# Fewer, longer runs of plain f32 instructions on TensorE in the token mixers of a two-layer streaming encoder

## The chip, the cores and the metric

The kernel runs on one core of a Trainium2 chip. The metric is the device time of one execution in microseconds (us). The five engines are called by the letters of the profile: PE (TensorE, with PEld for its weight loads), DVE (VectorE), ACT (ScalarE), POOL (GpSimd) and SP (SyncE, which issues most loads here).

## What is computed

The input `x` has 512 rows of 1024 values. There are two layers, each a token mixer and then a channel mixer (a gated MLP with a causal convolution of width 3), each with its residual, and a last norm. Layer A's mixer is an mLSTM of 4 heads (192 wide) beside memory attention; layer B's is band attention of 12 heads (64 wide) over keys and values that both come from layer A's output, beside memory attention. The three parts that the change touches, cut from the reference:

```python
# layer A: mLSTM output hm of each head, normalised over the head's 192 values
hm = hm * lax.rsqrt(jnp.mean(hm * hm, axis=-1, keepdims=True) + EPS)
...
# layer B: band attention of one chunk of 64 queries over 9 chunks of keys
s = jnp.einsum('bqhd,bkhd->bhqk', qc, kc) * scale + bias
p = jax.nn.softmax(jnp.where(valid, s, -jnp.inf), axis=-1)
return jnp.einsum('bhqk,bkhd->bqhd', p, vc)
...
# both layers: memory attention, 4 heads of 64 over 256 memory tokens
s = jnp.einsum('bshd,bmhd->bhsm', q, mk) * (MEM_HEAD_DIM ** -0.5)
return jnp.einsum('bhsm,bmhd->bshd', jax.nn.softmax(s, axis=-1), mv)
...
x = x + jnp.concatenate([mix_out, mem_out], axis=-1) @ w_out
```

## The kernel before, in words

Activations are held transposed: features on the 128 partitions, the 512 tokens along the free axis. A product in f32 is made of three products in the type fp32r: each operand is divided by `split` (L130) into a high part, a cast on ACT, and a low part, a subtraction on DVE, and `mm3` (L164) sums hi·hi, hi·lo and lo·hi, on lines L166, L167 and L168. So each tile of weights or activations that PE is to use passes through ACT and then DVE first. Tiles named `wr`, `wh`, `wl` are a load of weights and its two parts, `u` mostly activations and their parts, `pt` softmax weights in two parts, `t` work tiles, `s` small ones, `pmm`, `psc`, `ptr` the tiles of PSUM (3, 3 and 2 of them).

Some work on PE stays in plain f32: a transpose (L573, L1317) has the identity as one operand, and each mLSTM head has sums of squares against a matrix `mcf` of two columns (L1166, L1167).

The order of work in a mixer is written as generators. `weave(job, filler, each, lead)` takes a step of the job (a head, a pair of heads) and then as many steps of filler (projections, one `mm3` a step) as the job's `yield` has earned: `each` for a bare `yield`, `each` times the number for a numbered one. A scheduler then sets the order on each engine, with program order as priority and its own costs; each engine works in that order and waits where an operand isn't there.

- Memory attention (`memory_attention`, two heads at a time): scores on L504, softmax on L558 to L564 (maximum, exponential, reciprocal, and two normalising multiplies a head), for the first half of the queries and then for the second; `transposed(T2)` makes four transposes and a split for one head, yields, and does the same for the other; then the products with the values (L587, "PV" below) and `values`, L523 and L524, which adds the halves into a tile `t` that a split turns into the `u` pair that the output projection reads.
- Band attention (`band_attention`, six jobs of two heads): softmax of the query block T over T + 1 key blocks on L1302 to L1308, both heads, and `transposed(T)` with T + 1 transposes and a split for one head, then for the other. The steps stand in the order softmax 0, softmax 1, transposed 0, softmax 2, transposed 1, softmax 3, transposed 2, transposed 3, PV on L1338 and L1339.
- mLSTM heads (`mlstm_head`): the squares of both parts of the head go through ACT, four pairs of sums follow with a `yield 0.581` behind each, then a chain of small DVE instructions (L1171 to L1173, `rsqrt` L210, `diagonal` L221), a `yield 2.673`, and `spread` (L241), which PE needs the chain for.

Layer A weaves its four heads and the two pairs of memory attention one after another. Layer B weaves band jobs 0 to 3, memory pair 0, band job 4, and then, with the output projection `outp.part(...)` as filler, memory pair 1 and band job 5.

Of the kernel before, what the change touches and what calls it, by code (L numbers as in the profile page):

```python
# [12 lines left out]
AF = mybir.ActivationFunctionType  # L13
ALU = mybir.AluOpType
AX = mybir.AxisListType

P = 128
# [36 lines left out]
def trunk(  # L54
# [76 lines left out]
    def split(hi, lo, src, on_act=True, pinned=False):  # L131
        high = A.copy(hi, src) if on_act else V.tensor_copy(hi, src)  # L132
        low = V.tensor_tensor(out=lo, in0=src, in1=f(hi), op=ALU.subtract)  # L133
        if pinned:
            pin(high)
            pin(low)

    def load(src, a, b, extra=None):
# [67 lines left out]
    def until(there, filler):  # L206
        while not there():
            next(filler)

    def rsqrt(y, v):  # L210
# [331 lines left out]
    def memory_attention(q, kv, hp, mixes):  # L542
# [4 lines left out]
        ptl = [p[:, 2 * S : 4 * S].rearrange("p (a t) -> p a t", a=2) for p in pts]  # L547
        es = {}

        def softmax(T2):  # L550
# [5 lines left out]
            for h in range(2):  # L556
# [6 lines left out]
                for i in range(2):  # L563
                    V.tensor_scalar(e[:, i, :], e[:, i, :], sm[:, i : i + 1], None, op0=ALU.mult)  # L564
                es[T2, h] = e
                yield

        def transposed(T2):
            for h in range(2):
                tp = ps("tr").rearrange("p (a t c) -> p a t c", a=2, t=2)  # L570
                for i in range(2):
                    for a in range(2):
                        nc.tensor.transpose(tp[:, a, i, :], es[T2, h][:, i, a * P : (a + 1) * P], ident)  # L573
# [534 lines left out]
    def mlstm_head(h):  # L1108
# [48 lines left out]
        for o, j, r in ((nums[0], full, slice(0, P)), (nums[1], sh, rs)):  # L1157
            sq = sb("t", [P, S])
            A.activation(sq, o, AF.Square)
            sqs.append(sq)  # L1160
            V.tensor_tensor(out=og[j][r, :], in0=o[r, :], in1=og[j][r, :], op=ALU.mult)
        yield
        st = ps("sc")
        for T in range(TT):
            sl = slice(T * P, (T + 1) * P)
            nc.tensor.matmul(st[:, 2 * T : 2 * T + 2], sqs[0][:, sl], mcf[:, 0, :], start=True, stop=False)  # L1166
            nc.tensor.matmul(st[:, 2 * T : 2 * T + 2], sqs[1][:, sl], mcf[:, 1 + odd, :], start=False, stop=True)  # L1167
            yield 0.581
        st = st[:, : 2 * TT].rearrange("p (t c) -> p t c", c=2)
# [5 lines left out]
        dg = diagonal(fc)  # L1175
        yield 2.673
        fb = spread(dg, "sc")
# [107 lines left out]
    def band_attention(j, q, k, v):  # L1285
# [9 lines left out]
        def softmax(T):  # L1295
# [3 lines left out]
            for h in range(2):  # L1299
# [7 lines left out]
                V.reciprocal(sm, sm)  # L1307
                V.tensor_scalar(e, e, sm, None, op0=ALU.mult)  # L1308
                es[T, h] = e
            yield  # L1310

        def transposed(T):
            n = (T + 1) * P
            for h in range(2):
                tp = ps("tr")
                for b in range(T + 1):
                    nc.tensor.transpose(tp[:, b * P : (b + 1) * P], es[T, h][:, b * P : (b + 1) * P], ident)  # L1317
# [172 lines left out]
```

## Time and profile before

| | |
|---|---|
| runs, us | 1205.53, 1205.76 (median), 1206.40 |
| profiled execution, us | 1205.96 |
| its span, us | 1204.2 |
| PE, PEld, DVE, ACT, POOL busy share of the span | 99%, 88%, 79%, 58%, 10% |
| plain f32 matmuls of the kinds that the change touches | 360 |
| ACT table loads | 18 |

The span is from the first to the last instruction of the profiled execution; 1.8 us lie outside it. A time in the profile is counted from the start of the span. In a row of the timeline the first number is the start, the second the duration, the sign `x4` says that four like instructions were put together, and brackets give what the engine waited for just before. On PE the duration of a matmul is longer than the distance to the next one, because they overlap; the cost of one is therefore read from the distance of starts.

### The profile page before, as it was taken

The numbers are of one execution on the slowest core, as the hardware profiler recorded it, in microseconds if no ns is written. First come the engines' busy times: TensorE is split into PE (matmuls) and PEld (weight loads), VectorE is DVE, ScalarE is ACT, GpSimd is POOL, SyncE is SP. The second block draws the span as 40 slices with busy tenths as digits, with TensorE's granted clock in tenths as the row PEclk, the third lists the DMA queues.
The fourth block names the chain that finished last, engine by engine and source line by source line (L and its number), as shares of the span: only waits on it lengthen the run. The fifth ranks groups of instructions, "written<-read, shape, count | busy, mean of one in ns | idle before, by whom it ended". The sixth has DMA issues, their size and how long they took to land.

```text
span 1204.2 us, 18753 instructions
## 1 busy us (share of the span) xinstructions
PE 1192.6 (99%) x7047; PEld 1057.7 (88%) x7047; DVE 950.4 (79%) x1737; ACT 704.4 (58%) x1245; POOL 123.4 (10%) x207
## 2 busy tenths in 40 slices
PE   9999999999999999999999999999999999999997
PEld 9988888888889999999988888888889999999986
DVE  7878688778978877777698888997897877777755
ACT  4536577644555555555565667775455555555545
POOL 1300101000021111111020000001001010111100
PEclk9999999999999999999999999999999999999999
DMA  8634211454276666665563323246336466666551
GB/s 277 202 104 119 58 53 57 130 154 132 70 173 161 156 157 156 147 141 131 136 202 114 95 72 93 59 128 202 115 91 145 109 141 137 141 140 137 119 156 70
DMA packets 199020, 156.00 MB, mean 130 GB/s; under 512 B 7864, under 2 KB 179346, under 8 KB 198930
## 3 DMA queue, kind: packets, MB, share of 16 engines
q1 hardware_dynamic: 184338, 120.78, 34.3%
q0 software_dynamic: 14592, 34.03, 14.3%
q8 instruction: 55, 0.90, 0.3%
q14 instruction: 35, 0.29, 0.1%
HBM read 126.27 MB, written 32.44 MB: 132 GB/s over the span
## 4 chain that ended last, share of the span: by engine, by line
PE 93%; ACT 3%; DVE 3%; issue 1%; ACTq 0%; DVEq 0%
PE pmm L166 18%; PE pmm L167 17%; PE pmm L168 17%; PE ptr L166 6%; PE ptr L167 6%; PE ptr L168 6%; PE psc L166 5%; PE psc L167 5%; PE psc L168 5%; PE psc L504 2%; PE ptr L1317 1%; ACT wh L132 1%; PE ptr L1338 1%; PE ptr L1339 1%; ACT t L561 0%
## 5 line engine op out<-in xcount | busy, mean ns | idle before, releaser
L166 PE MATMUL pmm<-u,wh 128*128 128x512 f32 (+1 forms) x968 | 336.6, 348 | 0.1
L168 PE MATMUL pmm<-u,wl 128*128 128x512 f32 (+1 forms) x968 | 333.7, 345 | 0.0
L167 PE MATMUL pmm<-u,wh 128*128 128x512 f32 (+1 forms) x968 | 333.3, 344 | 0.1
L133 DVE TENSOR_TENSOR wl<-wr,wh 128x1024 fp32r<-128x1024 f32 (+4 forms) x174 | 201.9, 1161 | 103.0 <-ACT wh L132 102.4
L132 ACT CAST wh<-wr 128x1024 fp32r<-128x1024 f32 (+4 forms) x174 | 174.0, 1002 | 107.5 <-PE pmm L167 46.9
L168 PEld LDWEIGHTS pmm<-u,wl 128*128 128x128 f32 x968 | 183.6, 190 | 21.1
L167 PEld LDWEIGHTS pmm<-u,wh 128*128 128x128 f32 x968 | 183.9, 190 | 18.3 <-DVE u L133 0.8
L166 PEld LDWEIGHTS pmm<-u,wh 128*128 128x128 f32 x968 | 183.7, 190 | 18.1 <-ACT u L132 0.5
L166 PE MATMUL ptr<-u,wh 128*128 128x512 f32 x272 | 106.7, 392 | 0.0
L167 PE MATMUL ptr<-u,wh 128*128 128x512 f32 x272 | 106.5, 392 | 0.0
L168 PE MATMUL ptr<-u,wl 128*128 128x512 f32 x272 | 105.8, 389 | 0.0
L736 POOL DMA_DIRECT2D xspill<-t x64 | 55.5, 867 | 465.8 <-ACT t L735 455.4
L168 PE MATMUL pmm<-u,u 128*128 128x256 f32 x296 | 84.0, 284 | 0.2 <-DVE u L133 0.2
L166 PE MATMUL pmm<-u,u 128*128 128x256 f32 x296 | 84.2, 285 | 0.0
L167 PE MATMUL pmm<-u,u 128*128 128x256 f32 x296 | 83.8, 283 | 0.0
L133 DVE TENSOR_TENSOR u<-pt,u 128x512 fp32r<-128x512 f32 x102 | 70.2, 688 | 11.8 <-ACT u L132 9.2
L166 PE MATMUL psc<-u,wh 128*128 128x256 f32 (+1 forms) x232 | 76.1, 328 | 0.0
L168 PE MATMUL psc<-u,wl 128*128 128x256 f32 (+1 forms) x232 | 75.9, 327 | 0.0
L167 PE MATMUL psc<-u,wh 128*128 128x256 f32 (+1 forms) x232 | 75.9, 327 | 0.0
L735 ACT COPY t<-ptr 128x512 f32<-128x512 f32 x64 | 37.5, 586 | 60.4 <-PE ptr L168 60.4
L132 ACT CAST u<-pt 128x512 fp32r<-128x512 f32 x102 | 63.1, 619 | 11.4 <-DVE pt L845 11.3
L907 ACT ACTIVATE t<-t 128x512 f32<-128x512 f32 x34 | 21.6, 634 | 79.5 <-DVE t L644 79.5
(282 smaller groups left out, 2524.4 us busy)
## 6 DMA issues: line engine op xcount, KB each, us to landing
wr<-in_ffn_w_up_dram SPq DMA_DIRECT2D x54, 512.0 KB, 5.1
wr<-in_ffn_w_down_dram SPq DMA_DIRECT2D x38, 512.0 KB, 4.0
pt<-in_ffn_w_up_dram SPq DMA_DIRECT2D x34, 512.0 KB, 6.5
xspill<-t POOLq DMA_DIRECT2D x64, 256.0 KB, 4.9
wr<-in_a_w_in_dram SPq DMA_DIRECT2D x20, 512.0 KB, 3.7
xspill<-u POOLq DMA_DIRECT2D x32, 256.0 KB, 3.0
u<-xspill SPq DMA_DIRECT2D x32, 256.0 KB, 5.0
wr<-in_w_kv_dram SPq DMA_DIRECT2D x12, 512.0 KB, 4.0
```

What stands on the lines that cost most here:

```text
L132: high = A.copy(hi, src) if on_act else V.tensor_copy(hi, src)
L133: low = V.tensor_tensor(out=lo, in0=src, in1=f(hi), op=ALU.subtract)
L166: nc.tensor.matmul(o, lh, rh, start=first, stop=False, skip_group_check=more)
L167: nc.tensor.matmul(o, lh, rl, start=False, stop=False, skip_group_check=more)
L168: nc.tensor.matmul(o, ll, rh, start=False, stop=last, skip_group_check=more)
L504: nc.tensor.matmul(o, a, b, start=first and i == 0, stop=i == 1)
L735: A.copy(t, o)
L736: G.dma_start(xspill[j], t, accum_op=ALU.add)
L907: A.activation(self.acc, self.acc, AF.Silu)
L1317: nc.tensor.transpose(tp[:, b * P : (b + 1) * P], es[T, h][:, b * P : (b + 1) * P], ident)
L1338: nc.tensor.matmul(o2[:, s * P :], w, hi_at(pts[h], s, s, TT - s), start=s == 0, stop=False)
L1339: nc.tensor.matmul(o2[:, s * P :], w, lo_at(pts[h], s, s, TT - s), start=False, stop=s == TT - 1)
```

## The change

The instructions are the same, but for two more ACT table loads; their order is not. 84 stretches of plain f32 instructions on PE between fp32r ones become 51.

- `split` gives back its last instruction, and a helper `behind(i, *others)` makes instruction `i` wait for others.
- Memory attention: `transposed(T2)` takes both `ptr` tiles first and makes the eight transposes of both heads in succession; the first waits for the second head's last normalising multiply, and for the last split of the run before.
- Band attention: `transposed` takes several T. T = 0 and T = 1 become one run of both heads (2 · (1 + 2) transposes) behind softmax 2, with a bare `yield` more behind it; T = 2 and T = 3 are a run of both heads each. The first transpose waits for the second head's normalise.
- mLSTM: the eight sums stand in succession and the first waits for the last square; the `yield` behind the chain is 4.997, which is 2.673 + 4 · 0.581.

```diff
         def transposed(T2):
+            tps = [ps("tr").rearrange("p (a t c) -> p a t c", a=2, t=2) for _ in range(2)]
+            run_ = []
             for h in range(2):
-                tp = ps("tr").rearrange("p (a t c) -> p a t c", a=2, t=2)
+                e = es[T2, h][0]
                 for i in range(2):
                     for a in range(2):
-                        nc.tensor.transpose(tp[:, a, i, :], es[T2, h][:, i, a * P : (a + 1) * P], ident)
-                tsl = slice(2 * T2 * P, 2 * (T2 + 1) * P)
-                split(pth[h][:, :, tsl], ptl[h][:, :, tsl], tp.rearrange("p a t c -> p a (t c)"))
+                        run_.append(nc.tensor.transpose(tps[h][:, a, i, :], e[:, i, a * P : (a + 1) * P], ident))
+            behind(run_[0], es[T2, 1][1], *freed)
+            tsl = slice(2 * T2 * P, 2 * (T2 + 1) * P)
+            for h in range(2):
+                last = split(pth[h][:, :, tsl], ptl[h][:, :, tsl], tps[h].rearrange("p a t c -> p a (t c)"))
                 yield
+            freed.append(last)
...
-            nc.tensor.matmul(st[:, 2 * T : 2 * T + 2], sqs[0][:, sl], mcf[:, 0, :], start=True, stop=False)
+            i = nc.tensor.matmul(st[:, 2 * T : 2 * T + 2], sqs[0][:, sl], mcf[:, 0, :], start=True, stop=False)
+            if T == 0:
+                behind(i, last)
             nc.tensor.matmul(st[:, 2 * T : 2 * T + 2], sqs[1][:, sl], mcf[:, 1 + odd, :], start=False, stop=True)
-            yield 0.581
...
-        yield 2.673
+        yield 4.997
...
-        def transposed(T):
-            n = (T + 1) * P
-            for h in range(2):
-                tp = ps("tr")
-                for b in range(T + 1):
-                    nc.tensor.transpose(tp[:, b * P : (b + 1) * P], es[T, h][:, b * P : (b + 1) * P], ident)
-                split(
-                    blocks(pts[h], (T + 1) * P, 640, T + 1), blocks(pts[h], 3 * 640 + T * P, -768, T + 1),
-                    tp[:, :n].rearrange("p (b t) -> p b t", t=P),
-                )
+        def transposed(*Ts):
+            tps = [ps("tr") for _ in range(2)]
+            run_ = []
+            for T in Ts:
+                c = T * P if len(Ts) > 1 else 0
+                for h in range(2):
+                    e = es[T, h][0]
+                    for b in range(T + 1):
+                        run_.append(
+                            nc.tensor.transpose(tps[h][:, c + b * P : c + (b + 1) * P], e[:, b * P : (b + 1) * P], ident)
+                        )
+            behind(run_[0], es[Ts[-1], 1][1])
+            for T in Ts:
+                c = T * P if len(Ts) > 1 else 0
+                for h in range(2):
+                    split(
+                        blocks(pts[h], (T + 1) * P, 640, T + 1), blocks(pts[h], 3 * 640 + T * P, -768, T + 1),
+                        tps[h][:, c : c + (T + 1) * P].rearrange("p (b t) -> p b t", t=P),
+                    )
             yield
...
         yield from softmax(1)
-        yield from transposed(0)
         yield from softmax(2)
-        yield from transposed(1)
+        yield from transposed(0, 1)
+        yield
         yield from softmax(3)
```

Lines move with it: the helper's L166 to L168 become L167 to L169, memory transposes L573 become L583, memory PV L587 becomes L600, `values` L523 and L524 become L531 and L532, band softmax L1302 to L1308 become L1316 to L1322, band transposes L1317 become L1336, the sums L1166 and L1167 become L1179 and L1182, their chain L1171 to L1173 and L213 to L228 becomes L1185 to L1187 and L221 to L236, `spread`'s product L241 becomes L249.

The order changes in three places that are of interest. First, DVE behind the sums of the second mLSTM head: before, the chain's first instructions (on tiles `s`) alternate with taps of the convolution (L1075), and a split of weights stands ahead of them.

```order
L133 TENSOR_TENSOR wl_1875<-wr_1872,wh_1874 128x1024
L1075 SCALAR_TENSOR_TENSOR t_1694<-pmm_1628,cols_535,t_1694 128x511
L1171 TENSOR_TENSOR s_1726<-psc_1691,floor_592 128x4
L1075 SCALAR_TENSOR_TENSOR t_1694<-pmm_1628,cols_535,t_1694 128x510
L1172 TENSOR_SCALAR s_1726<-s_1726 128x4
```

After, in the same place:

```order
L1185 TENSOR_TENSOR s_1700<-psc_1691,floor_592 128x4
L1186 TENSOR_SCALAR s_1700<-s_1700 128x4
L1187 SCALAR_TENSOR_TENSOR s_1700<-psc_1691,s_1700 128x4
L221 TENSOR_SCALAR s_1701<-s_1700 128x4
L133 TENSOR_TENSOR wl_1875<-wr_1872,wh_1874 128x1024
L222 TENSOR_SCALAR s_1701<-s_1701 128x4
```

The taps have left the chain and the split of weights has come into it. On PE, 20 fp32r matmuls stand between the last sum and `spread` of this head after the change.

Second, PE at the end of layer A's memory pair 0, after the change (before, 15 matmuls stood between the last transposes and the first PV product):

```order
L583 MATMUL ptr_1961<-ident,t_1895 128x128 x4
L583 MATMUL ptr_1962<-ident,t_1910 128x128 x4
L167 MATMUL psc_2072<-u_1731,u_1783 128x512
L168 MATMUL psc_2072<-u_1732,u_1783 128x512
L169 MATMUL psc_2072<-u_1731,u_1784 128x512
L1132 MATMUL psc_2084<-u_894,sel_81 128x384
L600 MATMUL ptr_1984<-pt_1803,u_1270 128x512 x2
```

Four matmuls are left there. ACT, ahead of the same place, after the change (before, the two exponentials of L561 stand next to each other, with one table load behind them):

```order
L569 ACTIVATE t_1910,s_1908<-psc_1849,s_1907 128x256
L1089 ACT_TABLE_LOAD
L1089 ACTIVATE t_1854<-t_1854 128x512
L569 ACT_TABLE_LOAD
L569 ACTIVATE t_1910,s_1908<-psc_1849,s_1907 128x256
L493 ACTIVATE u_1860<-t_1854 64x512
L493 ACTIVATE u_1861<-t_1854 64x512
L496 CAST u_1860<-u_1860 64x512
L496 CAST u_1861<-u_1861 64x512
L132 CAST pt_1804<-ptr_1920 128x2x256
```

A silu of the convolution (L1089, on `t_1854`) with its table load, and another load back, have come between the two exponentials of a head; the first run's cast into `pt_1804`, whose split the second run of transposes waits for, stands behind.

Third, memory pair 1 of layer B with band job 5. PE, from the pair's PV to the first use of its result; before, 18 fp32r matmuls and two transposes stood between PV and the first use of its result, where now five matmuls stand, and the two heads' PV were six matmuls apart:

```order
L600 MATMUL ptr_8638<-pt_8523,u_7981 128x512 x2
L600 MATMUL ptr_8638<-pt_8523,u_7984 128x512 x2
L169 MATMUL pmm_8502<-u_8480,wl_8689 128x512
L512 MATMUL psc_8696<-u_8207,u_8318 128x256
L512 MATMUL psc_8696<-u_8207,u_8320 128x256
L512 MATMUL psc_8721<-u_8206,u_8317 128x384
L512 MATMUL psc_8721<-u_8206,u_8319 128x384
L167 MATMUL pmm_8500<-u_8649,wh_8768 128x512
L167 MATMUL pmm_8501<-u_8649,wh_8768 128x512
L167 MATMUL pmm_8502<-u_8649,wh_8768 128x512
L168 MATMUL pmm_8500<-u_8650,wh_8768 128x512
```

DVE before, from the second `values` sum (`t_8653`) to the low part of the result (`u_8660`); the next split of weights, 128x768, stands seven instructions behind it:

```order
L524 TENSOR_TENSOR t_8653<-ptr_8648,t_8654 64x512
L1307 RECIPROCAL s_8687<-s_8687 128x1
L1302 ISA t_8718,s_8719<-psc_8706,bias_8670 128x256
L1302 ISA s_8719 128x1
L1308 TENSOR_SCALAR t_8685<-t_8685,s_8687 128x128
L1307 RECIPROCAL s_8713<-s_8713 128x1
L133 TENSOR_TENSOR pt_8666<-ptr_8731,pt_8666 128x128
L133 TENSOR_TENSOR u_8660<-t_8653,u_8659 128x512
```

and after (`t_8643`, `u_8650`):

```order
L532 TENSOR_TENSOR t_8643<-ptr_8638,t_8644 64x512
L1321 RECIPROCAL s_8670<-s_8670 128x1
L1316 ISA t_8675,s_8676<-psc_8663,bias_8660 128x128
L1316 ISA s_8676 128x1
L1322 TENSOR_SCALAR t_8668<-t_8668,s_8670 128x128
L133 TENSOR_TENSOR wl_8895<-wr_8890,wh_8894 128x768
L133 TENSOR_TENSOR u_8650<-t_8643,u_8649 128x512
```

The split of weights now stands ahead of the low part, and PE uses that part sooner.

More of the change, by code (lines that the diff above doesn't have):

```diff
@@ L136, in split @@
             pin(low)
+        return low
     def load(src, a, b, extra=None):
@@ L208, in until, with behind @@
             next(filler)
+    def behind(i, *others):
+        for o in others:
+            tc.add_manual_dep(
+                i.ins, o.ins.name, mybir.DependencyInfo(mybir.DependencyClass.Sync, mybir.DependencyReason.DATA)
+            )
     def rsqrt(y, v):
@@ L547, in memory_attention @@
         ptl = [p[:, 2 * S : 4 * S].rearrange("p (a t) -> p a t", a=2) for p in pts]
-        es = {}
+        es, freed = {}, []
         def softmax(T2):
@@ L1158, in mlstm_head @@
             sq = sb("t", [P, S])
-            A.activation(sq, o, AF.Square)
+            last = A.activation(sq, o, AF.Square)
             sqs.append(sq)
@@ L1307, in softmax @@
                 V.reciprocal(sm, sm)
-                V.tensor_scalar(e, e, sm, None, op0=ALU.mult)
-                es[T, h] = e
+                last = V.tensor_scalar(e, e, sm, None, op0=ALU.mult)
+                es[T, h] = e, last
             yield
-        def transposed(T):
-            n = (T + 1) * P
-            for h in range(2):
-                tp = ps("tr")
-                for b in range(T + 1):
-                    nc.tensor.transpose(tp[:, b * P : (b + 1) * P], es[T, h][:, b * P : (b + 1) * P], ident)
-                split(
-                    blocks(pts[h], (T + 1) * P, 640, T + 1), blocks(pts[h], 3 * 640 + T * P, -768, T + 1),
-                    tp[:, :n].rearrange("p (b t) -> p b t", t=P),
-                )
+        def transposed(*Ts):
[16 more added lines that the diff above has]
+                        tps[h][:, c : c + (T + 1) * P].rearrange("p (b t) -> p b t", t=P),
+                    )
             yield
```

4 lines of the change are left out of this document (2 added, 2 removed).

## The prediction

> **What bounds the kernel now.** First the busy shares and the shares of the chain that ended last, then the two stretches that hold the edits, layer A's mixer and layer B's. In the rows of stretches the columns are the length, then busy time and count of PE, PEld, DVE, ACT and POOL, the granted clock, the DMA share and GB/s.
>
> ```profile
> PE 1192.6 (99%) x7047; PEld 1057.7 (88%) x7047; DVE 950.4 (79%) x1737; ACT 704.4 (58%) x1245; POOL 123.4 (10%) x207
> PE 93%; ACT 3%; DVE 3%; issue 1%; ACTq 0%; DVEq 0%
> ```
>
> ```profile
> 100.00:265.00 165.00, 164.60 (x842) 138.62 (x842) 126.96 (x259) 105.70 (x184) 12.35 (x25) 1.00 0.32 92
> 640.00:830.00 190.00, 189.17 (x979) 157.39 (x978) 160.22 (x399) 131.94 (x299) 14.72 (x26) 1.00 0.33 99
> ```
>
> PE is the bound: 93% of the chain, and in the two mixers it is idle for .40 and .83 us. Two things follow. All stalls that the change could remove there are worth 1.23 us at most; a gain beyond that must come from cheaper instructions on PE. And since PE is full, every us by which an operand is newly late is a us of the end. The granted clock is 1.00 in both, so nothing is to be had there. The time before is 1205.96 us for the profiled execution, .20 above the median; the sum is made against it and .20 taken off at the end. Under about .2% (2.4 us) a difference of this kernel can't be told from none.
>
> **a) The price of a run, 33 fewer.** What a run of plain f32 costs PE is read from the starts of the fp32r matmuls around it:
>
> ```profile
> 653.52 0.40 PE L168 MATMUL pmm<-u,wl 128*128 128x512 f32 x1
> 653.75 0.38 PE L1317 MATMUL ptr<-ident,t 128*128 128x128 f32 x2
> 653.89 0.47 PE L166 MATMUL pmm<-u,wh 128*128 128x512 f32 x1
> 654.21 0.39 PE L167 MATMUL pmm<-u,wh 128*128 128x512 f32 x1
> ...
> 660.21 0.82 PE L1317 MATMUL ptr<-ident,t 128*128 128x128 f32 x6
> 660.78 0.48 PE L166 MATMUL pmm<-u,wh 128*128 128x512 f32 x1
> 661.10 0.40 PE L167 MATMUL pmm<-u,wh 128*128 128x512 f32 x1
> ```
>
> An fp32r matmul of 512 columns is .23 (653.52 to 653.75). The one behind a run takes .32 (653.89 to 654.21), which looks like a price of .09 for each run. But two transposes together with that matmul are 653.75 to 654.21 = .46, less .23 = .23; six are 660.21 to 661.10 = .89, less .23 = .66. Four more cost .43, or .1075 each; two at that rate are .215, so .015 is left for the run as such: the first transposes take less (.14 for two) by what the matmul behind them takes more. The sums say the same:
>
> ```profile
> 126.91 0.28 PE L1166 MATMUL psc<-mcf,t 128*128 128x2 f32 x2
> 127.58 0.39 PE L167 MATMUL pmm<-u,wh 128*128 128x512 f32 x1
> 128.04 0.28 PE L1166 MATMUL psc<-mcf,t 128*128 128x2 f32 x2
> 129.17 0.39 PE L167 MATMUL pmm<-u,wh 128*128 128x512 f32 x1
> ```
>
> One step of four matmuls in two pairs is .67 − .23 = .44; two steps in succession are 1.13 − .23 = .90, against .88 for two apart, so −.02 for the run. Between −.02 and +.015 I take .005: 33 · .005 = .2, a gain. Ends: 33 · .015 = .5 gained, 33 · .02 = .7 lost.
>
> **b) mLSTM heads.** The sums no longer pause, and `yield 4.997` gives back the same filler behind the chain; but in the second head the split of weights 128x1024 now stands inside the chain.
>
> ```profile
> 248.64 0.16 DVE L1171 TENSOR_TENSOR s<-psc,floor 128x4 f32<-128x4 f32 x1 [0.51 <-PE psc L1167]
> 251.70 1.28 DVE L228 TENSOR_TENSOR t<-ident,s 128x512 fp32r<-128x512 f32 x2
> 800.99 1.23 DVE L133 TENSOR_TENSOR wl<-wr,wh 128x1024 fp32r<-128x1024 f32 x1 [0.25 <-ACT wh L132]
> ```
>
> Undisturbed (the last head) the chain runs from 248.64 to 252.34 with the first of the two diagonals (251.70 plus half of 1.28): 3.7. With the split it is 3.7 + 1.23 = 4.9, and with the hand-off from PE about 5.05. PE has 20 matmuls · .23 = 4.6 between the sums and `spread`. So +.45; ends 0 (the split finds a gap) and .9. The fourth head has a smaller split in it, 128x768, and as much work on PE: +.1.
>
> **c) Layer A, memory pair 0.** Two table loads more on ACT between the exponentials of one head, and 4 matmuls where 15 stood between the transposes and PV.
>
> ```profile
> 179.30 1.28 ACT L1076 ACT_TABLE_LOAD   x1
> 180.59 0.63 ACT L1076 ACTIVATE t<-t 128x512 f32<-128x512 f32 x1
> 184.26 1.06 ACT L132 CAST pt<-ptr 128x512 fp32r<-128x512 f32 x2
> 184.87 0.69 DVE L133 TENSOR_TENSOR pt<-ptr,pt 128x512 fp32r<-128x512 f32 x1 [0.24 <-ACT pt L132]
> 185.35 2.00 ACT L132 CAST wh<-wr 128x1024 fp32r<-128x1024 f32 x2
> 185.79 1.08 PE L587 MATMUL ptr<-pt,u 128*128 128x512 f32 x4
> ```
>
> Before, the cast began 1.5 before PV. Now a cast of weights (half of 2.00) stands ahead of it, and the low part is ready a cast and a subtraction behind the transposes (.59 and .69), which is 1.3, while PE gets there in 4 · .23 = .9: +.4 from that alone and, with the second load's 1.28 delaying the split that the run waits for, up to 1.3. I take +.5, ends 0 and 1.3. (The Trainium skill, "ScalarE: Activation LUTs", section "What ACT_TABLE_LOAD costs", gives a switch a load of about 1.28 us and a drain of about 1.38 us. This trace agrees on the load and shows no drain: 179.30 + 1.28 = 180.58, and the next instruction starts at 180.59. By the page two more loads would be 5.3 us of ACT and not 2.6, and the sum about 1211.6.)
>
> **d) Layer B, memory pair 0.**
>
> ```profile
> 762.05 0.86 DVE L564 TENSOR_SCALAR t<-t,s 128x256 f32<-128x256 f32 x2
> 762.91 0.60 PE L573 MATMUL ptr<-ident,t 128*128 128x128 f32 x4
> 767.33 0.57 ACT L132 CAST pt<-ptr 128x512 fp32r<-128x512 f32 x1
> 767.44 1.17 PE L587 MATMUL ptr<-pt,u 128*128 128x512 f32 x4
> ```
>
> The second head's normalise ended at 762.91 as its own transposes began; the first head's four stood ahead. Now both heads wait for it: +.2. PV again comes .7 behind the last transposes, where cast and subtraction are 1.3; +.6 with the other casts ahead, less the .4 that the same waits cost already in that stretch's .83. Together +.4, ends .2 and 1.0.
>
> **e) Band jobs 0 to 4.** Softmax 2 stands ahead of the first run, so its weights are ready sooner at T = 2. In the fifth job, which has the most filler, that ends the waits it had: −.4, within the .83 of that stretch; ends 0 and −.6. In jobs 0 to 3 the bare `yield` more keeps the distance, so nothing: the cover is their filler, 1.6 to 1.8 steps a yield, and were it gone the splits of T = 0 (.26 and .28) would be open, .5 a job.
>
> **f) Memory pair 1 with band job 5.** Here PE uses the pair's result five matmuls behind PV.
>
> ```profile
> 803.02 1.09 PE L587 MATMUL ptr<-pt,u 128*128 128x512 f32 x4
> 803.33 0.27 DVE L1302 CUSTOM_DVE_ANT_0 t<-psc,bias 128x128 f32<-128x128 f32 x1
> 803.54 0.28 DVE L1302 CUSTOM_DVE_ANT_0 t<-psc,bias 128x128 f32<-128x128 f32 x1
> 804.24 0.16 DVE L1307 RECIPROCAL s<-s 128x1 f32<-128x1 f32 x1 [0.41 <-ACT t L1306]
> 804.43 0.29 DVE L1308 TENSOR_SCALAR t<-t,s 128x128 f32<-128x128 f32 x1
> 805.09 0.69 DVE L524 TENSOR_TENSOR t<-ptr,t 64x512 f32<-64x512 f32 x1
> 806.68 0.68 DVE L133 TENSOR_TENSOR u<-t,u 128x512 fp32r<-128x512 f32 x1
> ...
> 767.28 0.95 DVE L133 TENSOR_TENSOR wl<-wr,wh 128x768 fp32r<-128x768 f32 x1
> ```
>
> PE, from the start of PV's second head to the first use of the low part: 4 of PV (.92), one (.23), two scores of 256 columns (.23) and two of 384 (.35), three of the high part (.69): 2.4. DVE from the same start: the second sum ends 805.09 + .69 − 803.02 = 2.76 behind it; then by the new order a reciprocal (.16), a softmax pass (.21 from start to start), a normalise (.21, likewise), the weights' split (.95) and the low part (.68), 4.97, of which overlaps of some .05 each come off: 4.7. Late by 4.7 − 2.4 = 2.3. Nothing hides it, since these rows of PE stand in order and what follows needs the same part. T = 0 and 1's run behind it waits too, but for work that is done meanwhile. Low end .5 (the two splits change places in time because the weights' cast is late anyway), high end 2.6 (no overlaps). By this PE waits on DVE near 805 to 808.
>
> **The sum.** −.2 + .45 + .1 + .5 + .4 − .4 + 2.3 = +3.15: 1209.1 on the profiled execution, 1208.9 on the median.
>
> **The rivals.**
> - *The waits are covered.* PE's queue may reach these places later than its count says, since each wait in front delays it and lets ACT and DVE catch up; f falls to .5, b and c to 0: −.2 + .1 + .4 − .4 + .5 = +.4, 1206.2: no change. For it: the 1.23 us of idle time before, so these engines have kept ahead so far. Against: 4.97 against 2.4 in f is far apart.
> - *The run has a price.* If the .09 of the matmul behind a run is paid for the run, 33 · .09 = 3.0 are gained; with the waits covered as in the rival above (+.6 without a) this gives 1205.76 − 3.0 + .6 = 1203.4, and if e takes its −.6 besides, 1203.2: faster. It decides from (2.4 + .6) / 33 = .09 a run. Against: the two-point line above, .015.
> - *It cascades.* Scores and softmax share three `psc` tiles; when PE stands at f, band job 5's next scores come late and its T = 2 waits once more for a whole softmax (about 1.1 by the pass, ACT and normalise rows above) in both later runs: 1208.9 + 2.2 and the high end of c: 1212.
>
> **How the numbers follow.** As summed .54, covered .28, a price of the run .12, cascade .06. The likeliest's own range is 1207.2 to 1211.5, by the ends of c, d and f. For the range, the faster case and the last part of the cascade are left out, with a little of the others: 1205.2 to 1211.8. Faster by over .2% (under 1203.35): most of the third case, .09. Slower (over 1208.17): .39 of the first, .06: .45. Within: the second, the first's lower part and the rest, .46.
>
> **What would show it.** PE idle in layer B's mixer up from .83 to about 3.5, most of it a wait on DVE for a low part `u` near 806; at `spread` of the second head a wait of about .45 for DVE's `t`; layer A's PV waiting for `pt`; the distances of starts around a run unchanged. Wrong it is if the matmul behind a long run and the run together take less than .1075 a transpose, or if PE does not wait at the pair's result.

## The result: slower by 5.5 us

The changed kernel takes 1211.34 us in the median of six runs (1210.93 to 1214.36), the kernel before 1205.80 in the same sessions (1205.36 to 1206.40): ratio 1.0052, 95% interval 1.0039 to 1.0065. That is 5.5 us, where 3.15 were forecast.

The profiled execution of the changed kernel is its slowest run, 1214.36 us with a span of 1212.4. It loses 3.0 us in its first 70 us, where nothing is changed, at a granted clock of .98 in the first 100 us against 1.00 before; so the two traces are compared only behind that. First the busy shares of the page, then the stretches, with the columns as in the prediction:

```profile
PE 1195.6 (99%) x7047; PEld 1058.8 (87%) x7047; DVE 950.0 (78%) x1737; ACT 706.3 (58%) x1247; POOL 121.8 (10%) x207
```

```profile
0.00:100.00 100.00, 94.67 (x568) 88.18 (x569) 76.50 (x171) 45.57 (x70) 13.69 (x43) 0.98 0.58 181
100.00:265.00 165.00, 163.74 (x833) 136.64 (x832) 124.56 (x256) 106.31 (x183) 9.82 (x22) 1.00 0.31 87
640.00:830.00 190.00, 186.90 (x964) 155.37 (x963) 158.35 (x397) 128.15 (x293) 12.92 (x24) 1.00 0.31 91
```

PE's idle time went from .40 to 1.26 us in layer A's mixer and from .83 to 3.10 in layer B's. PE's busy time over the whole execution did not fall (1192.6 us before, 1195.6 now); PE waits more.

For all that follows a sharper measure is used, the **lag**: PE has 7047 matmuls in every kernel here, and outside the two mixers the n-th is of the same kind in all. The difference of its start to that of before, less the same difference at the 500th (81.8 us in, ahead of the changes), is what was lost since. Two places are used, behind layer A's mixer (the 1600th, 305 us) and behind layer B's (the 4800th, 847 us). The changed kernel's lag is 1.93 us behind the first and 5.22 behind the second, so 1.93 are lost in layer A and 3.29 in layer B; from the 1600th to the 3700th, just ahead of layer B's mixer, it changes by .05, and from the 4800th to the end by .05. Inside a mixer the lag can be read too, at places where as many matmuls of each shape have gone by as before; the 880th, 940th, 1080th, 1270th and 1300th of layer A and the 4340th, 4440th, 4500th, 4550th and 4700th of layer B are such places.

**Where PE waits, layer A.** The first place is `spread` of the second mLSTM head:

```profile
157.37 0.17 DVE L221 TENSOR_SCALAR s<-s 128x4 int32<-128x4 int32 x1
157.44 1.22 DVE L133 TENSOR_TENSOR wl<-wr,wh 128x1024 fp32r<-128x1024 f32 x1
158.59 0.16 DVE L222 TENSOR_SCALAR s<-s 128x4 int32<-128x4 int32 x1
...
160.85 1.28 DVE L236 TENSOR_TENSOR t<-ident,s 128x512 fp32r<-128x512 f32 x2
161.04 0.39 PE L168 MATMUL pmm<-u,wh 128*128 128x512 f32 x1
161.59 0.50 PE L249 MATMUL psc<-t,onesr 128*128 128x512 f32 x1 [0.15 <-DVE t L236]
```

The split of weights stands between L221 and L222 as the order had it, and `spread` starts .55 behind the matmul ahead of it where .23 is the rule: .32 lost. (The bracket says less: it counts from the modelled end of the matmul ahead.) The matmul behind such a wait is late as well: it starts .34 behind and not .23 (161.59 to 161.92 here, 816.10 to 816.43 below), so a wait costs .11 more than its own length. The second place is the fourth head's scores, behind memory pair 1. Before, and then after:

```profile
234.16 1.09 PE L587 MATMUL ptr<-pt,u 128*128 128x512 f32 x4
235.69 0.58 ACT L523 COPY t<-ptr 64x512 f32<-64x512 f32 x1
236.30 1.16 ACT L1121 ACTIVATE t<-psc,acol 128x512 f32<-128x512 f32 x2
237.04 0.44 PE L166 MATMUL psc<-u,u 128*128 128x384 f32 x1 [0.21 <-ACT t L1121]
```

```profile
239.34 2.14 PE L600 MATMUL ptr<-pt,u 128*128 128x512 f32 x8
240.59 0.58 ACT L531 COPY t<-ptr 64x512 f32<-64x512 f32 x1 [0.74 <-PE ptr L600]
241.19 0.69 ACT L1134 ACTIVATE t<-psc,acol 128x512 f32<-128x512 f32 x1
241.93 0.44 PE L167 MATMUL psc<-u,u 128*128 128x384 f32 x1 [0.46 <-ACT t L1134]
...
243.14 0.39 PE L1132 MATMUL psc<-u,sel 128*128 128x256 f32 x1
...
245.01 0.50 PE L168 MATMUL ptr<-pt,u 128*128 128x512 f32 x1
```

ACT's exponential of the gates (L1134) reads a `psc` tile that PE needs back. It stands on ACT behind the copy of the pair's PV, and so waits for PV, which the long run of transposes has moved to just ahead of these scores: ACT is idle .74 us with that exponential in its queue. By starts the wait is .63 us (.37 before), and two more stand behind it, .23 at 243.14 and .28 at 245.01; from the 1270th to the 1300th matmul, which hold all three, the lag grows by 1.09.

**Layer B, the last stretch.** Memory pair 1's PV (L600) to the first use of its low part:

```profile
810.55 2.09 PE L600 MATMUL ptr<-pt,u 128*128 128x512 f32 x8
811.76 0.58 ACT L531 COPY t<-ptr 64x512 f32<-64x512 f32 x1 [0.17 <-PE ptr L600]
812.37 0.68 DVE L532 TENSOR_TENSOR t<-ptr,t 64x512 f32<-64x512 f32 x1 [1.31 <-ACT t L531]
812.98 0.27 DVE L1316 CUSTOM_DVE_ANT_0 t<-psc,bias 128x128 f32<-128x128 f32 x1
813.29 0.68 DVE L532 TENSOR_TENSOR t<-ptr,t 64x512 f32<-64x512 f32 x1
813.32 0.50 PE L512 MATMUL psc<-u,u 128*128 128x256 f32 x2 [0.44 <-DVE s L1316]
814.09 0.27 DVE L1316 CUSTOM_DVE_ANT_0 t<-psc,bias 128x128 f32<-128x128 f32 x1
814.43 0.62 PE L512 MATMUL psc<-u,u 128*128 128x384 f32 x2 [0.61 <-DVE s L1316]
814.49 0.95 DVE L133 TENSOR_TENSOR wl<-wr,wh 128x768 fp32r<-128x768 f32 x1
815.35 0.69 DVE L133 TENSOR_TENSOR u<-t,u 128x512 fp32r<-128x512 f32 x1
816.10 0.50 PE L168 MATMUL pmm<-u,wh 128*128 128x512 f32 x1 [0.35 <-DVE u L133]
```

PE waits three times, each time for DVE, but only the last is for the low part behind the weights' split. The first two are for softmax passes of band job 5 (L1316), each of which frees one of the three `psc` tiles. The passes' scores had been there before; DVE stood idle for 1.31 us at 812.37 with the first pass behind a value sum that waited for ACT's copy of PV. By starts the three come to .61, .77 and .52 us; with the .1 behind each of them the lag grows by 2.04 here (from the 4550th matmul to the 4700th).

**Layer B, memory pair 0**:

```profile
768.21 1.06 PE L583 MATMUL ptr<-ident,t 128*128 128x128 f32 x8 [0.21 <-DVE t L572]
...
774.84 2.11 PE L600 MATMUL ptr<-pt,u 128*128 128x512 f32 x8 [0.48 <-DVE pt L133]
```

Two waits, .37 and .65 us by starts, for the second head's normalise and for the low part of `pt`. The lag grows by .92 over the pair (from the 4340th matmul to the 4440th).

### The profile page after: what moved, and what is told of

Same layout as the page of the kernel before. It is cut to its first block, busy times and chain, and to the rows that moved or that the text cites. A ratio compares the mean times of both kernels' runs of the same rounds, so it can differ in the third digit from the quotient of the medians.

```text
span 1212.4 us, 18758 instructions
## 1 busy us (share of the span) xinstructions
PE 1195.6 (99%) x7047; PEld 1058.8 (87%) x7047; DVE 950.0 (78%) x1737; ACT 706.3 (58%) x1247; POOL 121.8 (10%) x207
## 4 chain that ended last, share of the span: by engine, by line
PE 91%; DVE 4%; ACT 3%; issue 1%; DMA 0%; SPq 0%; POOL 0%; DVEq 0%; ACTq 0%; POOLq 0%
PE pmm L167 17%; PE pmm L168 17%; PE pmm L169 17%; PE ptr L168 6%; PE ptr L167 6%; PE ptr L169 6%; PE psc L169 5%; PE psc L168 5%; PE psc L167 5%; PE psc L512 2%; PE ptr L1336 1%; PE ptr L1362 1%; ACT t L569 1%; PE ptr L600 1%; PE ptr L1363 1%
## 5 line engine op out<-in xcount | busy, mean ns | idle before, releaser
L167 PE MATMUL pmm<-u,wh 128*128 128x512 f32 (+1 forms) x968 | 335.1, 347 | 0.1
L168 PE MATMUL pmm<-u,wh 128*128 128x512 f32 (+1 forms) x968 | 333.0, 344 | 0.5 <-DVE u L133 0.3
L169 PE MATMUL pmm<-u,wl 128*128 128x512 f32 (+1 forms) x968 | 332.6, 344 | 0.0
L169 PEld LDWEIGHTS pmm<-u,wl 128*128 128x128 f32 x968 | 183.6, 190 | 21.0
L168 PEld LDWEIGHTS pmm<-u,wh 128*128 128x128 f32 x968 | 183.8, 190 | 19.9 <-DVE u L133 1.5
L167 PEld LDWEIGHTS pmm<-u,wh 128*128 128x128 f32 x968 | 183.6, 190 | 19.1 <-ACT u L132 0.5
L167 PE MATMUL ptr<-u,wh 128*128 128x512 f32 x272 | 106.7, 392 | 0.0
L168 PE MATMUL ptr<-u,wh 128*128 128x512 f32 x272 | 106.5, 392 | 0.0
L169 PE MATMUL ptr<-u,wl 128*128 128x512 f32 x272 | 105.8, 389 | 0.0
L169 PE MATMUL pmm<-u,u 128*128 128x256 f32 x296 | 84.4, 285 | 0.2 <-DVE u L133 0.2
L167 PE MATMUL pmm<-u,u 128*128 128x256 f32 x296 | 84.6, 286 | 0.0
L168 PE MATMUL pmm<-u,u 128*128 128x256 f32 x296 | 84.3, 285 | 0.0
L168 PE MATMUL psc<-u,wh 128*128 128x256 f32 (+1 forms) x232 | 76.0, 328 | 0.0
L169 PE MATMUL psc<-u,wl 128*128 128x256 f32 (+1 forms) x232 | 76.0, 327 | 0.0
L167 PE MATMUL psc<-u,wh 128*128 128x256 f32 (+1 forms) x232 | 75.9, 327 | 0.0
```

Source lines behind the costliest of these rows:

```text
L167: nc.tensor.matmul(o, lh, rh, start=first, stop=False, skip_group_check=more)
L168: nc.tensor.matmul(o, lh, rl, start=False, stop=False, skip_group_check=more)
L169: nc.tensor.matmul(o, ll, rh, start=False, stop=last, skip_group_check=more)
```

## The experiments

Each run is told with its own median and that of the kernel before in the same session, and with its lags: what was lost in layer A's mixer, and in layer B's. The changed kernel has 1.93 and 3.29.

### One part of the change at a time

`sums_only` has the mLSTM part of the diff alone, `mem_only` that of `memory_attention`, `band_only` that of `band_attention`, each with `behind` and the `return low` of `split`.

> Only the mLSTM part: the eight sums in succession and the yield of 4.997; all transposes as before. Theory (operands that come late): PE waits for the diagonal before the second head's spread as in the changed kernel, +.3 to +.5 us there, less some .1 us for twelve fewer runs; in all +.2 to +.6 us against the kernel before, and no change in layer B. Rival (a run of f32 has a price of its own that fewer runs save): 12 fewer runs at .09 us gain 1.1 us, the time falls by about .6 us. Rival (the heads' part also causes the wait of .46 us at the fourth head's scores): +1.4 us.

> Only memory attention's part: both heads' transposes in one run in all four pairs; sums and band jobs as before. Theory (late operands behind these runs): layer A +.4 us at pair 0's PV and up to +1.0 us at the fourth head's scores, layer B +.8 us at pair 0, and in the last stretch between 0 and +1.9 us, by whether the pair's runs alone bring its PV close to the first use; in all +2 to +4 us. Rival (the band jobs' runs cause the loss of the last stretch): +1 to +2 us in all and nothing in the last stretch.

> Only the band jobs' part: T = 0 and 1 in one run, T = 2 and T = 3 with both heads in one; sums and memory attention as before. Theory (the memory pair's runs cause the loss of the last stretch): +.3 to +.8 us, from jobs 0 to 4 alone. Rival (band job 5's later first run lets PE reach the pair's result too early): +2 to +2.5 us, most of it in the last stretch with waits for a low part or for softmax passes.

| kernel | us | before | lag layer A | lag layer B |
|---|---|---|---|---|
| sums_only | 1207.06 | 1206.01 | .86 | -.10 |
| mem_only | 1208.83 | 1206.01 | 1.40 | .97 |
| band_only | 1208.26 | 1206.01 | -.05 | 1.95 |
| sum of the three | | | 2.21 | 2.82 |
| all three, the changed kernel | 1211.34 | 1205.80 | 1.93 | 3.29 |

Ratios: 1.0008 (.9999 to 1.0018), 1.0023 (1.0014 to 1.0033), 1.0019 (1.0009 to 1.0028). No part gains, and no part carries it all. By its times `sums_only` can't be told from no change (its interval reaches below 1), so its loss is read from the lag. The rival of a saved price per run has no support in it: it forecast a gain. The clean test, without the new waits, is `sums_y6` below. (The expectation counted twelve fewer runs. A head's sums stood in two or three runs already, eleven in all, so there are seven fewer, and .6 us at .09 a run.) That part lost more than was expected of it (.86 against at most .6): .44 at `spread` of the second head (880th to 940th matmul), and another .43 from there to the 1080th, some 170 to 199 us in. The wait at the fourth head's scores is memory attention's: in `mem_only` it is .63 us by starts, as in the changed kernel. In the last stretch the theory was wrong in `band_only`: not the memory pair's runs but the band jobs' part alone lost 1.60 us there, as its rival had it, with waits by starts of .53 us at scores and of .26 and .35 at the pair's high and low part. On DVE the 128x768 split stands ahead of the low part there too. The rest of `band_only`'s loss is mostly in jobs 0 to 3, with .29. The memory pairs' part alone (`mem_only`) lost .37 in the last stretch, and .91 at layer B's pair 0.

### Layer B's memory pair 1 apart again

```diff
-    weave(memory_attention(memq[1], memkv, 1, mixes), fill, 0.48, 4)
+    weave(memory_attention(memq[1], memkv, 1, mixes, (False, False)), fill, 0.48, 4)
```

(with a second `transposed` in `memory_attention`, that of before, taken where the flag is False).

> The changed kernel with one part undone: layer B's memory pair 1 makes its four transposes a head apart, as before; everything else stays changed. Theory (that pair's runs cause the loss of the last stretch): the waits for softmax passes and the low part near the end of layer B's mixer go, -1.5 to -1.9 us against the changed kernel, so 1209.5 to 1209.9. Rival (band job 5's merged run causes it): the waits stay, and the time stays at about 1211.3.

1209.99 us; lag 1.88 and 1.43. Layer B's loss falls by 1.86, as expected, and all of it in the last stretch (.11 is lost there, where it was 2.04). The three waits are gone, though job 5 keeps its long runs; the order has now four matmuls of filler between PV and the next scores and three between those and the ones after, and the low part stands ahead of the weights' split:

```profile
807.92 0.27 DVE L1326 CUSTOM_DVE_ANT_0 t<-psc,bias 128x128 f32<-128x128 f32 x1
808.23 0.69 DVE L532 TENSOR_TENSOR t<-ptr,t 64x512 f32<-64x512 f32 x1
808.32 0.44 PE L512 MATMUL psc<-u,u 128*128 128x256 f32 x2
...
809.37 0.62 PE L512 MATMUL psc<-u,u 128*128 128x384 f32 x2
...
809.77 0.69 DVE L133 TENSOR_TENSOR u<-t,u 128x512 fp32r<-128x512 f32 x1
```

Seen beside `band_only`, in which this pair is apart too and 1.95 us are lost, it is not the pair's long run as such that costs. What differs is the order: where filler stands on PE, and where passes, sums and the weights' split stand on DVE. The scheduler settles that anew for each variant.

### The last stretch taken apart: the low part, and the passes

`lo_first` keeps the low part of the pair's result ahead of the weights' split, by a fixed order of the two (`values` has `pinned` for layer B's pair 1 alone; the condition on the weights holds in both layers); `soft_first` issues job 5's first softmax ahead of the pair's PV.

```diff
-        split(hi, lo, s)
+        split(hi, lo, s, pinned=pinned) 
...
-            wh, wl = weights([...], len(ks), (j1 - j0) * P)
+            raw = load([...], len(ks), (j1 - j0) * P)
+            wh, wl = parts(raw, pinned=g == 1 and ks[0] == 3)
```

```diff
+    pair = memory_attention(memq[1], memkv, 1, mixes)
+    weave(islice(pair, 12), fill, 0.48, 4)
     job = band_attention(5, *qkv.pop(5))
+    next(job)
+    weave(pair, fill, 0.48)
     fill = chain(fill, outp.part(0, 7))
-    weave(islice(job, 8), fill, 2.372)
+    weave(islice(job, 7), fill, 2.372, 2.372)
```

> The changed kernel; in the last stretch only the place of one split of weights is moved: the low part of the memory pair's result stands ahead of the 128x768 split on DVE, as before the change. Theory (three waits in a row there, for two softmax passes that stand behind the pair's value sums on DVE and free score tiles, and for the low part behind the weights' split): the wait of .5 us for the low part goes or falls under .2, the two waits of .4 and .6 us for the passes stay; about 1210.8 us. Rival (the weights' split is the whole loss of the stretch, as the prediction had it): all three go, -1.5 us or more, about 1209.7 us.

> The changed kernel; band job 5's first softmax is issued ahead of the memory pair's products with the values, so two softmax passes stand ahead of the value sums on DVE and not behind them. Theory (the scores wait for tiles that passes behind the value sums free): the first of the two waits goes, the second becomes a wait of some .3 us for a later pass, and the low part is used three matmuls later, so its wait falls: -.5 to -1.0 us, 1210.3 to 1210.8 us. Rival (the passes don't matter, only the low part): the low part's wait stays at about .5 us and the time at about 1211.3 us.

`lo_first`, timeline of the same place:

```profile
811.52 0.50 PE L512 MATMUL psc<-u,u 128*128 128x256 f32 x2 [0.47 <-DVE s L1317]
812.63 0.62 PE L512 MATMUL psc<-u,u 128*128 128x384 f32 x2 [0.61 <-DVE s L1317]
...
813.03 0.69 DVE L133 TENSOR_TENSOR u<-t,u 128x512 fp32r<-128x512 f32 x1
...
814.14 0.40 PE L168 MATMUL pmm<-u,wh 128*128 128x512 f32 x1
```

The wait for the low part is gone, and the two for the passes stand as they were (.63 and .77 by starts): the theory holds at this place, and the prediction's picture of one wait falls. The total was a miss: 1218.06 us against 1205.83, not 1210.8, with lags of 3.39 and 8.70. The same flag fixes the order of a split in layer A's output projection too. PE waits 1.67 us for weights (`wh`) there, at 257.24, and again later in layer B, behind the stretch in question:

```profile
829.36 0.50 PE L167 MATMUL psc<-u,wh 128*128 128x512 f32 x1 [2.25 <-ACT wh L132]
```

`soft_first` came to 1210.96 us against 1205.83, lags 1.85 and 2.86. The three waits fall to .35, .73 and .18 us by starts, from .61, .77 and .52; the passes do matter. But the first wait was expected to go and falls by less than half, and the second was expected at .3 and hardly moved, so what sets the second is not shown. The gain in layer B is .43, a little under the .5 to 1.0 expected.

### The fourth head's scores, and the second head's spread

`fourth_apart` sets layer A's memory pair 1 apart as `pair_apart` did layer B's. `yield6`:

```diff
-        yield 4.997
+        yield 6.0
```

> The changed kernel with one part undone: layer A's memory pair 1 makes its four transposes a head apart, as before. Theory (PE reaches the pair's products with the values sooner behind its transposes, and ACT does the decay of the fourth head behind the copy of those products, so the fourth head's scores wait for it): the wait of .46 us at these scores and the two behind it go, -1.0 to -1.2 us at that place, about 1210.2 us. Rival (the heads' longer yield causes it): the waits stay, about 1211.3 us.

> The changed kernel with the yield behind the mLSTM heads' chain at 6.0 and not 4.997, which puts 28 fp32r matmuls and not 20 between the second head's sums and its spread. Theory (the chain with a split of weights in it takes 4.9 us where PE has 4.6): the wait at spread goes, -.3 to -.5 us at that place. Rival (the chain is late for another reason, and grows with the filler): the wait stays at .3 us or more.

`fourth_apart`: 1210.49 us, lags .91 and 3.36, so 1.02 less in layer A. It is won at this place: from the 1270th to the 1300th matmul the lag stays as it is (-.01), where it grew by 1.09. Its row:

```profile
237.62 0.44 PE L167 MATMUL psc<-u,u 128*128 128x384 f32 x1 [0.18 <-ACT t L1144]
```

The wait is that of before (.21).

`yield6`: 1212.55 us in three runs (1212.09 to 1214.35), 1.2 above the changed kernel where a gain was expected. Part of that may lie behind the mixers: in the profiled execution it is 8.12 us from the last matmul's start to the end of the span, where the changed kernel has 7.21. Why is not known. The lags are 1.33 and 3.26, so .60 less in layer A. But that is not `spread` alone:

```profile
161.56 0.50 PE L249 MATMUL psc<-t,onesr 128*128 128x512 f32 x1
187.48 2.00 PE L600 MATMUL ptr<-pt,u 128*128 128x512 f32 x8
```

At `spread` the wait falls from .32 to .11, and the lag there grows by .22 where it grew by .46: a gain of .24, a little under the .3 to .5 expected. The edit does more than add cover. On DVE three taps of the convolution are back in the chain, which takes 5.91 us from L1185 to L236 and not 4.08. On ACT the program has 16 table loads and not 20, the two exponentials of a head of memory pair 0 stand next to each other again, and the pair's first PV product starts without a wait, where the changed kernel waits .44. So this run takes two causes away in part, and does not by itself show that the split of weights made the chain late; that rests on the rows above, where the split takes 1.22 us between two instructions of the chain.

### Layer B's memory pair 0 apart

> The changed kernel with layer B's memory pair 0 apart, all else changed. Theory (this pair's merged runs cost .9 us at their own waits, of which .5 us come back in band job 4, where work that was moved is saved): -.4 us over the two together; in the last stretch the waits for softmax passes stay, and the low part now stands ahead of the weights' split, so its wait goes: another -.5 us; about 1210.4 us. Rival (the pair's loss is a plain loss): -.9 us there.

1210.36 us against 1206.11, lags 1.87 and 1.86: layer B's loss falls by 1.43, more than the .9 expected of the two places. The wait at the pair's PV is gone, that of its transposes back to .15. The lag no longer grows over the pair (-.01, from .92), and the next band job does not give .5 back (.09 more from the 4440th matmul to the 4550th, .06 in the changed kernel): the pair's loss is a plain one, as the rival had it, and the time near 1210.4 was met by another sum than the theory's. In the last stretch the two waits for passes stay (.85 and .77 us by starts) and the one for the low part is gone, worth .48 of lag. That an edit at 765 us takes away a wait at 816, with 40 us of other work between, comes by the order again: here too the low part now stands ahead of the weights' split.

### Three causes at once, and what is left of the sums

`three_undone` is `fourth_apart`, `pair_apart` and `yield6` in one; `sums_y6` is `sums_only` with the yield at 6.0.

> The changed kernel with three causes taken away together: layer A's memory pair 1 and layer B's memory pair 1 make their transposes a head apart, and the yield behind the heads' chain is 6.0; the other runs stay long. Theory (three separate waits, which add up: about -1.0, -1.7 and -.6 us): 1207.5 to 1208.2 us, no waits of PE at the second head's spread, at the fourth head's scores beyond the .3 us that they had before, or at the last stretch's low part. Rival (a wait that is removed comes back at the next place, since PE arrives earlier there): 1209 us or more.

> Only the mLSTM part of the change, with the yield at 6.0: the sums in long runs, and their chain no longer waited for; all transposes as before. Theory (a run has a price of about .01 us, so twelve fewer save .1 us and the wait was all that the part cost): 1205.5 to 1206.0 us, no difference from the kernel before. Rival (a run costs .09 us): 1.1 us faster, about 1204.8 us.

`three_undone`: 1208.08 us against 1206.11 (ratio 1.0016, 1.0007 to 1.0025), lags .39 and 1.54. The single gains in lag were 1.02, 1.86 and .60, together 3.48; both lags together fell from 5.22 to 1.93, by 3.29. They add up nearly, so these are separate losses and not one that moves on; the third of them, the longer yield, is more than one wait. Of the 1.5 us left in layer B, .29 are in band jobs 0 to 3, .92 in memory pair 0, .05 in the fifth job, the last stretch has .07, and .24 are lost behind it. `sums_y6`: 1206.22 against 1206.11, ratio 1.0000 (.9991 to 1.0010), lags .21 and -.13. Here the lag at the 1080th matmul is .14, where `sums_only` has .80. Without these waits the part is worth nothing that can be measured. The run of sums in it:

```profile
127.13 0.28 PE L1174 MATMUL psc<-mcf,t 128*128 128x2 f32 x2
...
128.83 0.47 PE L167 MATMUL pmm<-u,wh 128*128 128x512 f32 x1
129.15 0.39 PE L168 MATMUL pmm<-u,wh 128*128 128x512 f32 x1
```

Sixteen matmuls in one run take 129.15 − 127.13 − .23 = 1.79. Before, six runs of four took .45 each and five of eight .895, all sums 7.2 us; now four runs take 1.80 each, 7.2 again: nothing that the trace resolves is saved by seven runs fewer. The two lags together, .08, hold no gain of .6 us either.

## Why the prediction was half right

The time (1211.34) is near the upper end of the range (1205.2 to 1211.8), and the sum (+3.15) had the right sign but was short by 2.4 us; the chance of no measurable change (.46) stood just above that of slower (.45), and slower it was. The mechanism, operands that come late on a full PE, was right; three places in the sum were not. Where the changed kernel's lag grows, beside the terms:

| place (matmuls) | term | forecast | lag grows by |
|---|---|---|---|
| second head's `spread` (880 to 940) | b | .45 | .46 |
| behind it, with memory pair 0 (940 to 1270) | c | .5 | .33 |
| memory pair 1, fourth head's scores (1270 to 1300) | none | | 1.09 |
| rest of the fourth head (1300 to 1600) | b | .1 | .10 |
| band jobs 0 to 3 (3700 to 4340) | e | 0 | .29 |
| layer B's memory pair 0 (4340 to 4440) | d | .4 | .92 |
| fifth job, the wait that it had (4440 to 4500) | e | -.4 | -.44 |
| fifth job, its last run (4500 to 4550) | e | 0 | .50 |
| last stretch (4550 to 4700) | f | 2.3 | 2.04 |

The steps that failed are the missing term for layer A's memory pair 1 (1.09), e, which comes to +.35 and not to -.4, and d, with .92 for .4. Together these three are 2.4 short, of which c and f give .4 back; what the runs save is in the lags already. Term by term:

- **a, the price of a run.** Right: .2 us of gain was forecast, .005 a run. From the runs of both traces that have no wait in them, less .2275 for the matmul behind, one transpose costs .114 us, two .223, three .333, four .442, six .660, eight .878: .109 each and .005 for the run. One run of six in place of two of one and two of two saves .014, one of eight in place of two of four .006, all transposes together some .2. The rival that counted the .09 of the matmul behind a run fell with `sums_y6`.
- **b, the second head.** Right: .45 forecast, .46 at `spread`, of which .32 are the wait and .11 the matmul behind it. `yield6` took .24 of it away, not .60.
- **c, layer A's pair 0.** Near: +.5 forecast, .33 measured. At the first PV product PE waits .44 by starts, while a wait of .22 that stood before at scores nearby (190.52) is gone. The two more table loads did run (180.41 and 182.36, 1.28 each). They come with the mLSTM part of the change, not with the pair's: `sums_only` has 20 loads, `mem_only` 18. Neither of these two runs has the wait at PV, so as far as they show it takes both parts. In the rows below, of the changed kernel, the next instruction starts .01 to .02 behind each load, and the instruction ahead of each ends .02 before it. The drain that the Trainium skill gives with such a load ("ScalarE: Activation LUTs", "What ACT_TABLE_LOAD costs") does not show here, so that the sum with it, 1211.6, lies near the measured time is luck.

```profile
180.41 1.28 ACT L1089 ACT_TABLE_LOAD   x1
181.71 0.63 ACT L1089 ACTIVATE t<-t 128x512 f32<-128x512 f32 x1
182.36 1.28 ACT L569 ACT_TABLE_LOAD   x1
183.65 0.47 ACT L569 ACTIVATE t<-psc,s 128x256 f32<-128x256 f32 x1
```

- **Missing: layer A's memory pair 1.** The largest fault. The parts of the prediction have no term for the fourth head's scores behind that pair; the long runs there cost 1.02 us (`fourth_apart`). The wait was in the trace of before already, with .21 of idle time and the same releaser, ACT's L1121 behind the copy of PV; a place where PE already waits is one where a later operand costs in full.
- **d, layer B's pair 0.** Under-sized: +.4 forecast, with 1.0 as its high end, and .92 measured, all of which goes when the pair is set apart. Its own waits rose from .16 at the transposes and .08 at PV to .37 and .65. The prediction took off .4 for what these waits cost already; they cost .24.
- **e, band jobs 0 to 4.** Half right. The fifth job's wait did end, as forecast: before, its run at 783.71 waits .32 by starts, and -.44 of lag come there. But its last run waits .48 at 795.18 for the second head's normalise, which the first transpose of a long run now needs, and the lag grows by .50. Jobs 0 to 3, put at nothing, lose .29, with new waits of .14 at 670.63 and .25 at 740.99.
- **f, the last stretch.** The size was right (2.04 for 2.3), the path mostly not. The low part was ready 816.04 − 811.47 = 4.6 us behind the start of PV's second head (forecast 4.7; PV's eight matmuls start at 810.55, so the second head's at 811.47), and PE, which needed 2.4 us of its own work, used it at 4.6. So 2.2 were lost by this count. But 1.4 of them were lost ahead, at two waits for `psc` tiles, only .5 at the low part, and .3 at the matmuls behind these waits. Most of layer B's new idle time was to stand at the low part; of the 3.10 us idle it has .35 by its bracket. That the size came out in spite of this is in part luck. The prediction had that mechanism only in its smallest rival (the cascade, .06), as an extra price and not as the way in which f's time is paid. `lo_first` tells them apart.

The rival that had the waits covered was given .28 on the ground that the engines had kept ahead before, with 1.23 us idle in both mixers. None of the summed waits was covered: b, c, d and f all came. That share, with the lower part of the first case, is what put "no change" ahead of "slower".

What stays open: the .43 that `sums_only` loses behind `spread`, which goes with the longer yield of `sums_y6` but has several small waits; the cause of the waits in band jobs 0 to 3; and what sets the second wait of the last stretch. None of the three was tested by itself.

## What to carry to other kernels

Where one engine is full, price a grouping of instructions twice: what the group saves on that engine, read from the starts around short and long runs, and what the operands of the next steps then wait for. Look for the second in the queues of the helping engines: an instruction that frees a buffer, and is ready, may stand behind one that waits for the moved work, and the full engine then waits for the buffer. A list of such waits starts with the places where the profile of before shows a small wait already, since there every delay counts in full; the last stretch of layer B had none before, so the list does not end there. And an experiment that adds cover also changes the order: look at what else moved before its gain is put down to one wait.

## What the runs showed that was not expected

A change of order early in a program altered the order 40 us later: setting apart layer B's memory pair 0 moved the low part of pair 1's result ahead of a weights' split, and its wait of .5 us went. A part's cost measured alone (`band_only` 1.95 us in layer B, `pair_apart` 1.43 with the same job 5) is therefore the cost of one order, and the parts of layer B do not add as simply as the three causes of `three_undone` do. Fixing the order of two instructions by hand in `lo_first` did what it should at its place and cost some 7 us elsewhere (its two lags are 12.1 us together against 5.2).
